# A conformer block with dilated attention on one Trainium2 core: hand order for the first norms, conv result split in pieces, early splits of the last projection

## The chip, the cores and the metric

The kernel runs on one core of one Trainium2 chip. A core has a matrix engine (TensorE, PE in the profile, with its weight loads as PEld), a vector engine (DVE), an activation engine (ACT), GpSimd (POOL) and SyncE (SP), whose queue issues nearly all transfers here. Each engine takes its instructions in order, and semaphores tie the engines together. The metric is the device time of one execution in microseconds (us), as the median of several runs. Lower is better.

## The reference

One layer of a block over 1024 tokens of width 1024, all in float32:

```
h = rms_norm(x, norm1_g);  z = h @ w_in            # glu 2048 | q 1024 | k 1024 | v 1024 | gates 2048
a = a_val * sigmoid(a_gate)                        # the two halves of glu
a = causal_depthwise_conv(a, conv_w, conv_b)       # width 31
y_a = silu(rms_norm(a, conv_norm_g)) @ w_conv_out
o = 16 heads of 64: softmax over windows (128,1), (512,4), (2048,16), merged by their sums
y_b = o @ w_attn_out
x = x + (g_a * y_a + g_b * y_b) @ w_out            # g_a, g_b: sigmoid of the gates
h = rms_norm(x, norm2_g);  u = causal conv of width 3 over h @ w_up   # 2 * 2816 channels
x = x + (silu(u_gate) * u_val) @ w_down
```

## The kernel before

**Splits.** TensorE gets each float32 operand as two parts in a faster format: a high part, which ACT copies (line 76), and a low part, source minus high part, which DVE subtracts (line 77). `split` (line 74) issues both. A product of two operands is three matmuls: high by high, high by low, low by high (lines 108 to 110, 125 to 127, 550 to 552, 703). `stage` (line 79) loads a weight piece of 128 x 1024 into one of four buffers (tag "raw"), `wsplit` (line 84) splits it into tags "whi" and "wlo" with four buffers each, and `wpiece` (line 90) does both.

**The order of the instructions.** The context is made with `schedule_with_timeline_sim=True` (line 855): while the kernel is built, instructions are put in order on each engine, and the order in which the program asks for them is only the priority. So an instruction asked for late may stand early in its engine's queue if its inputs and its buffer are free in the builder's model.

**First norms (lines 197 to 224).** The eight tiles of x (128 tokens x 1024) are loaded (line 204); two weight pieces are asked for after the fourth, g0 and v0 of the first channel tile (line 207), with their splits. The norm's weight g1 is loaded to all 128 partitions by one transfer on ACT's queue (line 200). For each tile: squares and their sum on ACT (line 221), `rstd_of` (line 98: one scalar step on DVE, line 100, and a power on POOL, line 101), scaling by the root and g1 on DVE (line 223), and `transpose_split` (line 183): two PSUM banks with four transposes each (line 190), each bank then split into hT. hT lies in four buffers of pool hb1: high and low part for each half of 512 tokens.

**Channel tiles (lines 227 to 238).** For each of eight tiles c: 48 matmuls of the gate columns (`glug`), a sigmoid, 48 of the value columns (`gluv`), and a product. All 48 of one go through both halves of the tokens. Then come q, k and v (lines 301 to 313), 24 columns of gates, the long convolution on DVE (line 253), its norm, and the store of the result to DRAM as `da` (line 340).

**Heads with side work (lines 345 to 470).** Sixteen heads, each in two halves. PE alternates between scores, transposes of the weights, and products with v; the weights' transposes are split by ACT and DVE as well (`flip`, line 396). `fill` (line 415) takes steps from a generator, `side_work` (line 346), and puts them between a head's instructions. One step is three matmuls of one k. The side work is the rest of the gate columns, the last four in two halves of 32 steps each, and then the projection of the conv result, w_co, eight columns by two halves. That projection reads aT, the split of `da`, and aT takes the buffers of hT half by half: the first half at the mark "half" of `gate_steps` (line 163), the second when all gates are done. Each `load_split` (line 165) loads and splits four pieces of 128 x 1024 at once (lines 350 and 352). The four weights of a group are asked for after them (line 354).

**Up projection and last projection.** The up projection runs over 22 tiles f (lines 655 to 659): `up_first` (line 557), `up_sums` (line 566), `up_rest` (line 623), which ends with a store to `dff` (line 653). The last projection (lines 664 to 804) reads it back in groups of two tiles (`gload`, line 673), loads w_down (`wload`, line 679), splits both (`gsplit`, line 686; `wsplit`) and multiplies (`mac`, line 696) in the seven products of a Strassen-like scheme. The operands of the first two groups go into two buffers named `early` (line 664) of pool hb2, under the tags that held the left operands of `up_first`.

Of the kernel before, what the change touches and what calls it, by code (L numbers as in the profile page):

```python
# [12 lines left out]
F32 = mybir.dt.float32  # L13
F32R = mybir.dt.float32r
# [6 lines left out]
P = 128  # L21
# [4 lines left out]
DH = 64  # L26
# [24 lines left out]
def block_kernel(ctx: ExitStack, tc: tile.TileContext, x, g1, g2, pack, mask,  # L51
# [13 lines left out]
    def bank_ps(name):  # L65
        return psB.tile([P, 512], F32, tag="B", name=name)
# [116 lines left out]
    def transpose_split(dst, src, tt):  # L183

        half, c0 = tt // 4, (tt % 4) * P
        for kk in range(2):
            ps = bank_ps(f"tp_{tt}_{kk}")
            for j in range(4):
                k = kk * 4 + j
                pe.transpose(ps[:, j * P : (j + 1) * P], src[:, k * P : (k + 1) * P], ident)  # L190
            psv = ps.rearrange("p (a b) -> p a b", a=4)
            hi = dst[0][half][:, kk * 4 : kk * 4 + 4, c0 : c0 + P]
            lo = dst[1][half][:, kk * 4 : kk * 4 + 4, c0 : c0 + P]
            split(hi, lo, psv)


    with tc.tile_pool(name="ph1", bufs=1) as p1:
        t4 = lambda name, dt=F32: p1.tile([P, 1024], dt, tag="t4", bufs=4, name=name)
        gb1 = p1.tile([P, D], F32, tag="csq", bufs=1, name="gb1")
        act.dma_start(gb1, bass.AP(tensor=g1.tensor, offset=g1.offset, ap=[[0, P], [1, D]]))  # L200
# [7 lines left out]
        sp.dma_start(pk, pack)  # L208
        make_identity(nc, ident)
        pool.memset(mhalf, -0.5)  # L210
        pool.memset(ones, 1.0)
        dve.tensor_tensor(out=qkg, in0=pk[:, C_QG : C_QG + 1], in1=pk[:, C_KG : C_KG + 1], op=ALU.mult)
        dve.tensor_scalar(qkg, qkg, DH ** -0.5, None, op0=ALU.mult)

        hT = hb_tiles(hb1, "hT")
        for tt in range(8):
            xx = xt[tt]
            xs = t4(f"xs_{tt}")
            ss = p1.tile([P, 1], F32, tag="ss", bufs=2, name=f"ss_{tt}")
            rs = p1.tile([P, 1], F32, tag="rs", bufs=2, name=f"rs_{tt}")  # L220
            act.activation(xs, xx, AF.Square, accum_out=ss)
            rstd_of(rs, ss, D, ss)
            dve.scalar_tensor_tensor(out=xs, in0=xx, scalar=rs, in1=gb1, op0=ALU.mult, op1=ALU.mult)
            transpose_split(hT, xs, tt)
# [3 lines left out]
        for c in range(8):  # L228
            a = p1.tile([P, CW - 1 + T], F32, tag="apad", bufs=10, name=f"apad_{c}")
            pool.memset(a[:, : CW - 1], 0.0)  # L230
            gp = big_ps(f"glug_{c}")
            gemm_ch(gp, wfirst[0] if c == 0 else wpiece(w_ch[8 + c], f"g{c}"), hT)
            sg = t4(f"sg_{c}")
            act.activation(sg, gp, AF.Sigmoid)
            vp = big_ps(f"gluv_{c}")
            gemm_ch(vp, wfirst[1] if c == 0 else wpiece(w_ch[c], f"v{c}"), hT)
            dve.tensor_tensor(out=a[:, CW - 1 :], in0=vp, in1=sg, op=ALU.mult)
            apad.append(a)

        sqacc = p1.tile([P, T], F32, name="sqacc")  # L240
# [104 lines left out]
    with tc.tile_pool(name="ph2", bufs=1) as p2:  # L345
        def side_work():
            for t in gates:
                if t == "half":
                    aT = hb_tiles(hb1, "aT")
                    load_split(aT, da, 0, "a")  # L350
                yield
            load_split(aT, da, 1, "a")
            for c0 in (0, 4):
                ws = [wpiece(w_co[c], f"co{c}") for c in range(c0, c0 + 4)]
                for half in range(2):
                    for c in range(c0, c0 + 4):
                        yp = bank_ps(f"ya_{c}_{half}")
                        yield from gemm_half(yp, ws[c - c0], aT, half)
                        ya = cst.tile([P, 512], F32, tag="f2", bufs=2, name=f"ya_{c}_{half}")
                        act.activation(ya, yp, AF.Copy)  # L360
                        sp.dma_start(dya[c][:, half * 512 : half * 512 + 512], ya)
# [249 lines left out]
    with tc.tile_pool(name="ph4", bufs=1) as p4:  # L611
# [52 lines left out]
    early = [hb2.tile([P, 3, 1024], F32R, tag=f"hb{a}1", name=f"early{a}") for a in range(2)]  # L664
    with tc.tile_pool(name="ph5", bufs=1) as p5_:
        HF, G = FT // 2, 2
        groups = [range(f, min(f + G, HF)) for f in range(0, HF, G)]
# [11 lines left out]
        def wload(k, j, fs, pl=p5_):  # L679
            raw = pl.tile([P, G * 512], F32, tag="wr" if pl is p5_ else "raw", bufs=4,  # L680
                          name=f"wr{k}{j}_{fs[0]}")[:, : len(fs) * 512]
            sp.dma_start(raw.rearrange("p (f d) -> p f d", d=512),
                         w_down[k * HF + fs[0] : k * HF + fs[-1] + 1, :, j * 512 : j * 512 + 512].rearrange("f p d -> p f d"))
            return raw

        def gsplit(src, name, dst=None):
            n = src.shape[1]
            if dst is not None:
                split(*dst, src)
                return dst  # L690
# [28 lines left out]
        for fs in groups:  # L719
            e = early.pop(0) if early else None  # L720
            g = gload(0, 0, fs, dst=None if e is None else e[:, 0].bitcast(F32))
# [21 lines left out]
        for fs in groups:  # L743
            s2, t2 = part("s2", fs), part("t2", fs)
            first, last = fs is groups[0], fs is groups[-1]
            a21, a22, a11 = wload(0, 1, fs), wload(1, 1, fs), wload(0, 0, fs, wp)
# [10 lines left out]
        for fs in groups:  # L757
            s2, t2 = part("s2", fs), part("t2", fs)
            first, last = fs is groups[0], fs is groups[-1]
            a12, a11, a21 = wload(1, 0, fs, wp), wload(0, 0, fs), wload(0, 1, fs)  # L760
# [16 lines left out]
        for fs in groups:  # L777
            s2, t2 = part("s2", fs), part("t2", fs)
            first, last = fs is groups[0], fs is groups[-1]
            a12, a22, b21 = wload(1, 0, fs, wp), wload(1, 1, fs), gload(1, 0, fs)  # L780
# [78 lines left out]
```

## Time and profile before

| what | value |
|---|---|
| median of 3 runs | 1812.32 us (1812.14 to 1815.67) |
| the profiled execution, its own time | 1811.43 us |
| its span, first to last instruction | 1809.6 us |
| mean granted TensorE clock | 0.991 |
| PE busy, 0 to 45 us | 31.64 us |
| PE busy, 90 to 600 us | 506.27 of 510 us |
| PE busy, 600 to 1140 us | 527.73 of 540 us |
| PE busy, 1140 to 1300 us | 150.66 of 160 us |
| PE busy, 1640 to 1809 us | 166.07 of 169 us |

How to read the profile: a row of a group names line, engine, operation, what it writes and reads, shapes and count, then busy us and the mean ns of one, then the idle time ahead of it and what ended it. A row of the order of time starts with the start in us and the duration; with a count behind x, the duration is that of the whole row. A row of a table of stretches gives the stretch, its length, then for PE, PEld, DVE, ACT and POOL the busy us and (x) the instructions begun, then the granted clock, the share of the transfer engines and GB/s. SPq and ACTq are the queues that issue transfers. Matmuls overlap, so a row's duration is longer than the distance between two.

### The profile page before, as it was taken

The numbers are of one execution on the slowest core, as the hardware profiler recorded it, in microseconds if no ns is written. First come the engines' busy times: TensorE is split into PE (matmuls) and PEld (weight loads), VectorE is DVE, ScalarE is ACT, GpSimd is POOL, SyncE is SP. The second block draws the span as 40 slices with busy tenths as digits, with TensorE's granted clock in tenths as the row PEclk, the third lists the DMA queues.
The fourth block names the chain that finished last, engine by engine and source line by source line (L and its number), as shares of the span: only waits on it lengthen the run. The fifth ranks groups of instructions, "written<-read, shape, count | busy, mean of one in ns | idle before, by whom it ended". The sixth has DMA issues, their size and how long they took to land.

```text
span 1809.6 us, 22474 instructions
## 1 busy us (share of the span) xinstructions
PE 1765.8 (98%) x8244; PEld 1461.9 (81%) x8244; DVE 1318.8 (73%) x1798; ACT 771.6 (43%) x1202; POOL 195.8 (11%) x197
## 2 busy tenths in 40 slices
PE   7999999999999999999999999989999999999999
PEld 5888888888887888887888878768888888878887
DVE  5999999999735655666654543787777777789863
ACT  4111132232245656666655332545444554543441
POOL 1000133133002122222210000210000000000000
PEclk9999999999999999999999999999999999999999
DMA  5111145345549456666527543313222222389851
GB/s 203 59 47 47 41 134 163 116 134 157 157 173 246 145 158 175 180 165 179 164 70 279 169 160 133 104 48 107 80 82 81 71 95 91 116 303 335 298 180 47
DMA packets 142063, 257.57 MB, mean 142 GB/s; under 512 B 11265, under 2 KB 60545, under 8 KB 141953
## 3 DMA queue, kind: packets, MB, share of 16 engines
q1 hardware_dynamic: 141808, 255.61, 43.8%
q8 instruction: 65, 1.06, 0.3%
q10 hardware_dynamic: 144, 0.52, 0.1%
q14 instruction: 46, 0.37, 0.1%
HBM read 190.03 MB, written 66.06 MB: 142 GB/s over the span
## 4 chain that ended last, share of the span: by engine, by line
PE 53%; DMA 4%; DVE 4%; issue 1%; ACT 1%; SPq 1%; POOLq 0%; POOL 0%; DVEq 0%; ACTq 0%
PE xz L550 5%; PE xz L551 5%; PE xz L552 5%; PE dx L703 5%; PE dy L703 5%; DMA gg<-dya 2%; PE pp L400 2%; PE y L550 2%; PE y L552 2%; PE y L551 2%; PE ya L108 2%; PE ya L109 2%; PE ya L110 2%; PE o L408 2%; PE wo L126 1%; PE wo L127 1%
## 5 line engine op out<-in xcount | busy, mean ns | idle before, releaser
L253 DVE SCALAR_TENSOR_TENSOR cacc<-apad,pk,cacc 128x1024 f32<-128x1024 f32 x240 | 297.7, 1274 | 0.7
L125 PE MATMUL qkv<-hi_qkv,hT 128*128 128x512 f32 x384 | 151.8, 396 | 0.0
L127 PE MATMUL qkv<-hi_qkv,hT 128*128 128x512 f32 x384 | 150.0, 391 | 0.0
L126 PE MATMUL qkv<-lo_qkv,hT 128*128 128x512 f32 x384 | 149.4, 390 | 0.0
L389 DVE CUSTOM_DVE_ANT_0 p<-s,m 128x128 f32<-128x128 f32 (+7 forms) x128 | 95.1, 750 | 62.7 <-PE pp L400 39.0
L77 DVE TENSOR_TENSOR pl<-pp,ph 128x512 fp32r<-128x512 f32 x192 | 103.1, 549 | 49.1 <-ACT ph L76 48.6
L393 POOL TENSOR_SCALAR p<-p,st 128x128 f32<-128x128 f32 (+7 forms) x128 | 94.9, 748 | 335.5 <-DVE st L392 211.9
L76 ACT ACTIVATE ph<-pp 128x512 fp32r<-128x512 f32 x192 | 91.3, 487 | 92.2 <-PE pp L400 89.3
L649 DVE SCALAR_TENSOR_TENSOR u<-u,pk 128x1023 f32<-128x1023 f32 (+1 forms) x88 | 112.3, 1279 | 18.9 <-ACT u L647 18.5
L101 POOL TENSOR_TENSOR rs<-ss,mhalf 128x8 f32<-128x8 f32 (+1 forms) x40 | 80.3, 2010 | 353.1 <-DVE ss L100 353.0
L391 ACT ACTIVATE p<-p,st 128x128 f32<-128x128 f32 (+7 forms) x128 | 99.0, 776 | 14.6 <-DVE st L389 12.9
L108 PE MATMUL gate<-hT,hi_gt 128*128 128x512 f32 x256 | 101.8, 398 | 0.0
L109 PE MATMUL gate<-hT,hi_gt 128*128 128x512 f32 x256 | 100.8, 394 | 0.0
L110 PE MATMUL gate<-hT,lo_gt 128*128 128x512 f32 x256 | 100.3, 393 | 0.0
L400 PE MATMUL pp<-ident,p 128*128 128x128 f32 x576 | 94.4, 277 | 0.0
L127 PEld LDWEIGHTS qkv<-hi_qkv,hT 128*128 128x128 f32 x384 | 72.0, 188 | 15.3
L126 PEld LDWEIGHTS qkv<-lo_qkv,hT 128*128 128x128 f32 x384 | 72.2, 188 | 14.5 <-DVE lo_qkv L77 0.3
L125 PEld LDWEIGHTS qkv<-hi_qkv,hT 128*128 128x128 f32 x384 | 72.2, 188 | 14.0
L400 PEld LDWEIGHTS pp<-ident,p 128*128 128x128 f32 x576 | 69.5, 142 | 10.0 <-issue 0.2
L384 PE MATMUL s<-kh,q 128*128 128x512 f32 (+1 forms) x192 | 69.7, 368 | 7.3 <-DVE st L389 4.8
L408 PE MATMUL o<-ph,v 128*128 128x512 f32 x192 | 73.1, 381 | 3.6 <-ACT ph L76 1.8
L409 PE MATMUL o<-pl,v 128*128 128x512 f32 x192 | 70.5, 369 | 1.6 <-DVE pl L77 1.5
(269 smaller groups left out, 4610.4 us busy)
## 6 DMA issues: line engine op xcount, KB each, us to landing
wr<-w_down SPq DMA_DIRECT2D x45, 512.0 KB, 5.7
gr<-dff SPq DMA_DIRECT2D x62, 256.0 KB, 5.2
raw_qkv<-w_qkv SPq DMA_DIRECT2D x24, 512.0 KB, 3.9
raw_uv<-w_up SPq DMA_DIRECT2D x22, 512.0 KB, 3.3
raw_ug<-w_up SPq DMA_DIRECT2D x22, 512.0 KB, 3.3
dff<-u SPq DMA_DIRECT2D x22, 512.0 KB, 2.6
dv<-v SPq DMA_DIRECT2D x16, 512.0 KB, 3.2
raw_gt<-w_ch SPq DMA_DIRECT2D x16, 512.0 KB, 4.8
```

The source lines that it names most:

```text
L108: pe.matmul(o, hi[:, k, :], ah[:, k, :], start=(k == 0), stop=False)
L109: pe.matmul(o, hi[:, k, :], al[:, k, :], start=False, stop=False)
L110: pe.matmul(o, lo[:, k, :], ah[:, k, :], start=False, stop=(k == KT - 1))
L125: pe.matmul(ps, ah, hi[:, k % 2, :], start=(k == 0), stop=False)
L126: pe.matmul(ps, ah, lo[:, k % 2, :], start=False, stop=False)
L127: pe.matmul(ps, al, hi[:, k % 2, :], start=False, stop=(k == KT - 1))
L253: dve.scalar_tensor_tensor(out=acc, in0=a[:, j : j + T], scalar=w(j), in1=acc, op0=ALU.mult, op1=ALU.add)
L400: pe.transpose(pp[:, qb * P : (qb + 1) * P], pts[qb][:, kt * P : (kt + 1) * P], ident)
L550: pe.matmul(o, wh[:, k, :], bh[:, k, :], start=(start and k == 0), stop=False, skip_group_check=not start)
L551: pe.matmul(o, wh[:, k, :], bl[:, k, :], start=False, stop=False, skip_group_check=not start)
L552: pe.matmul(o, wl[:, k, :], bh[:, k, :], start=False, stop=(k == 3), skip_group_check=not start)
L703: pe.matmul(banks[n], a[:, c], b[:, d], start=(start and i == 0 and m == 0), stop=(stop and i == nf - 1 and m == 2), skip_group_check=True)
```

## The change

It has three parts.

**First norms in a hand order.** The order of ACT, DVE and PE in this stretch is fixed by `tc.manual_schedule`. g1 is loaded as one row, multiplied by a row of ones on PE into two banks, and copied by DVE into gb1. All four squares of the first half come first; the scalar step of a tile stands after the scaling of the tile two before it, in the second half after the scaling of the tile one before. Transposes, high and low parts are issued bank by bank. The products of channel tile 0 are taken apart (`first_pair`): the first half of the tokens begins with k 0 to 3 as soon as the first banks of tiles 0 to 3 are split, and the transposes of tiles 4 to 7 stand between the products. Gate and value columns of one half share one two-bank PSUM tile. Sigmoid and product of tile 0 go by halves. The weights of channel tile 1 are asked for behind the last high and low part, and so are the two small instructions for qkg.

**Conv result in pieces.** A piece of the first half of aT is asked for at the mark and then every seventh step of side work; the pieces of the second half are asked for one ahead of each of the first four column products, behind the weights w_co.

**Early splits.** The loads and splits into `early` are asked for ahead of the last `up_rest`, no longer in the first pass of the last projection; `wload` and the groups move up with them.

The core of the diff:

```diff
-    def load_split(dst, src, half, name):
-        for k in range(0, KT, 2):
+    def load_split(dst, src, half, name, ks=range(0, KT, 2)):
+        for k in ks:
...
-        gb1 = p1.tile([P, D], F32, tag="csq", bufs=1, name="gb1")
-        act.dma_start(gb1, bass.AP(tensor=g1.tensor, offset=g1.offset, ap=[[0, P], [1, D]]))
+        g1r = p1.tile([1, D], F32, tag="csq", bufs=1, name="g1r")
+        act.dma_start(g1r, g1.unsqueeze(0))
...
-                wfirst = [wpiece(w_ch[8], "g0"), wpiece(w_ch[0], "v0")]
+                wfirst = [(c, n, stage(w_ch[c], n)) for c, n in ((8, "g0"), (0, "v0"))]
...
+        glu0 = [big_ps("glugv_0"), None]
+        third = big_ps("tp_2")
...
+        def both(tt, kk):
+            return high(tt, kk), low(tt, kk)
+        def first_pair(half, ks, passes, which):
+            o = glu0[half][:, which * 512 : which * 512 + 512]
+            for wa, ha in passes:
+                for k in ks:
+                    pe.matmul(o, wfirst[which][wa][:, k, :], hT[ha][half][:, k, :],
+                              start=(k == 0 and (wa, ha) == (0, 0)), stop=(k == 7 and (wa, ha) == (1, 0)))
...
+        HH, HL, LH = ((0, 0),), ((0, 1),), ((1, 0),)
+        with tc.manual_schedule(engines={ENG.Activation, ENG.DVE, ENG.PE}):
+            ps = [bank_ps(f"gb_{kk}") for kk in range(2)]
+            for kk in range(2):
+                pe.matmul(ps[kk], ones[0:1, :], g1r[:, kk * 512 : kk * 512 + 512], start=True, stop=True)
+            for tt in range(4):
+                squares(tt)
+            dve.tensor_copy(gb1[:, 0:512], ps[0])
+            spread1(0)
+            dve.tensor_copy(gb1[:, 512:1024], ps[1])
+            spread1(1)
+            for tt in range(4):
+                scaled(tt)
+                turned(tt)
+                if tt < 2:
+                    spread1(tt + 2)
+                if tt == 2:
+                    both(0, 0)
+            both(0, 1)
+            both(1, 0)
+            both(2, 0)
...
+            act.activation(hl[0][0], wraw[0], AF.Copy)
+            both(3, 0)
+            act.activation(hl[1][0], wraw[1], AF.Copy)
+            wlow(0)
+            wlow(1)
+            a, b = range(4), range(4, 8)
+            first_pair(0, a, HH, 0)
+            first_pair(0, a, HH, 1)
+            first_pair(0, a, HL + LH, 0)
+            first_pair(0, a, HL + LH, 1)
+            squares(4)
+            spread1(4)
+            both(1, 1)
+            both(2, 1)
+            both(3, 1)
+            squares(5)
+            scaled(4)
+            spread1(5)
+            first_pair(0, b, HH, 0)
+            turned(4)
+            first_pair(0, b, HH, 1)
+            squares(6)
+            scaled(5)
+            spread1(6)
+            turned(5)
+            first_pair(0, b, HL + LH, 0)
...
+            ends = both(7, 1)
+        for ks in (a, b):
+            for which in range(2):
+                first_pair(1, ks, HH + HL + LH, which)
...
+        with tc.issue_after(ends[0].ins), tc.issue_after(ends[1].ins):
+            wsecond = [wpiece(w_ch[9], "g1"), wpiece(w_ch[1], "v1")]
...
                 if t == "half":
                     aT = hb_tiles(hb1, "aT")
-                    load_split(aT, da, 0, "a")
+                    left = list(range(0, KT, 2))
+                    wait = 0
+                elif left:
+                    if wait == 0:
+                        load_split(aT, da, 0, "a", [left.pop(0)])
+                    wait = (wait + 1) % 7
                 yield
-            load_split(aT, da, 1, "a")
+            left = list(range(0, KT, 2))
             for c0 in (0, 4):
                 ws = [wpiece(w_co[c], f"co{c}") for c in range(c0, c0 + 4)]
                 for half in range(2):
                     for c in range(c0, c0 + 4):
+                        if left:
+                            load_split(aT, da, 1, "a", [left.pop(0)])
...
         for f in range(FT):
+            if f == FT - 1:
+                for a, fs in enumerate(groups[:2]):
+                    e = hb2.tile([P, 3, 1024], F32R, tag=f"hb{a}1", name=f"early{a}")
+                    for i, k in enumerate(fs):
+                        sp.dma_start(e[:, 0, i * 512 : i * 512 + 512].bitcast(F32), dff[k][:, 0:512])
+                    split(e[:, 1], e[:, 2], e[:, 0].bitcast(F32))
+                    early.append((e[:, 1], e[:, 2]))
             up_rest(f, *ready.pop(0))
...
-            mac(X, gsplit(g, f"b11_{fs[0]}", None if e is None else (e[:, 1], e[:, 2])), wsplit(w, f"a11_{fs[0]}"), len(fs), fs is groups[0], fs is groups[-1])
+            g = early.pop(0) if early else gsplit(gload(0, 0, fs), f"b11_{fs[0]}")
+            mac(X, g, wsplit(w, f"a11_{fs[0]}"), len(fs), fs is groups[0], fs is groups[-1])
```

The new helpers not shown are the old instructions under names: `squares` (line 221 of before), `spread1` (`rstd_of`), `scaled` (line 223), `turned` (two banks of transposes), `high` and `low` (the two halves of a split of one bank), `wlow` (the low part of a weight).

More of the change, by code (lines that the diff above doesn't have):

```diff
@@ L215, in block_kernel @@
         hT = hb_tiles(hb1, "hT")
[L216 to L224, printed above, removed]
+        glu0 = [big_ps("glugv_0"), None]
@@ new lines, in block_kernel, with squares, spread1 @@
+        third = big_ps("tp_2")
+        gb1 = p1.tile([P, D], F32, tag="sqacc", bufs=1, name="gb1")
+        xn = [t4(f"xs_{tt}") for tt in range(4)]
+        st1 = p1.tile([P, 2, 8], F32, name="st1")
+        tps = {}
+        def squares(tt):
+            if tt >= 4:
+                xn.append(t4(f"xs_{tt}"))
+            act.activation(xn[tt], xt[tt], AF.Square, accum_out=st1[:, 0, tt : tt + 1])
+        def spread1(tt):
+            rstd_of(st1[:, 1, tt : tt + 1], st1[:, 0, tt : tt + 1], D, st1[:, 0, tt : tt + 1])
@@ new lines, in scaled, with turned @@
+        def scaled(tt):
+            dve.scalar_tensor_tensor(out=xn[tt], in0=xt[tt], scalar=st1[:, 1, tt : tt + 1], in1=gb1,
+                                     op0=ALU.mult, op1=ALU.mult)
+        def turned(tt):
+            for kk in range(2):
+                ps = third[:, kk * 512 : kk * 512 + 512] if tt == 2 else bank_ps(f"tp_{tt}_{kk}")
+                for j in range(4):
+                    k = kk * 4 + j
+                    pe.transpose(ps[:, j * P : (j + 1) * P], xn[tt][:, k * P : (k + 1) * P], ident)
+                tps[tt, kk] = ps.rearrange("p (a b) -> p a b", a=4)
@@ new lines, in part, with high, low @@
+        def part(tt, kk, a):
+            half, c0 = tt // 4, (tt % 4) * P
+            return hT[a][half][:, kk * 4 : kk * 4 + 4, c0 : c0 + P]
+        def high(tt, kk):
+            return act.activation(part(tt, kk, 0), tps[tt, kk], AF.Copy)
+        def low(tt, kk):
+            return dve.tensor_tensor(out=part(tt, kk, 1), in0=tps[tt, kk], in1=part(tt, kk, 0).bitcast(F32),
+                                     op=ALU.subtract)
+        def both(tt, kk):
+            return high(tt, kk), low(tt, kk)
@@ L661, in block_kernel @@
     p4r_cm.__exit__(None, None, None)
-    early = [hb2.tile([P, 3, 1024], F32R, tag=f"hb{a}1", name=f"early{a}") for a in range(2)]
     with tc.tile_pool(name="ph5", bufs=1) as p5_:
-        HF, G = FT // 2, 2
-        groups = [range(f, min(f + G, HF)) for f in range(0, HF, G)]
         keep3 = {}
@@ L677, in gload, with gsplit @@
             return raw[:, : len(fs) * 512]
[L679 to L686, printed above, removed]
+        def gsplit(src, name):
             n = src.shape[1]
-            if dst is not None:
-                split(*dst, src)
-                return dst
             hi = p5_.tile([P, G * 512], F32R, tag="gh", bufs=4, name=f"gh_{name}")[:, :n]
```

82 lines of the change are left out of this document (56 added, 26 removed).

## The prediction

> **What bounds the kernel now.** I read the page first, then the waits of TensorE (PE), then a table of stretches, and last the order of time where PE stands still.
>
> ```profile
> span 1809.6 us, 22474 instructions
> ```
> and, from its first part,
>
> ```profile
> PE 1765.8 (98%) x8244; PEld 1461.9 (81%) x8244; DVE 1318.8 (73%) x1798; ACT 771.6 (43%) x1202; POOL 195.8 (11%) x197
> ```
> PE is busy for 1765.8 of 1809.6 us. An edit of order can win only in the 43.8 us of idle PE, and where PE is busy at a lower clock. The table says where these are (stretch, its length, busy us by engine, then PEclk):
>
> ```profile
> 0.00:45.00 45.00, 31.64 (x148) 25.62 (x149) 24.94 (x38) 22.08 (x38) 7.00 (x24) 0.92 0.53 204
> 90.00:600.00 510.00, 506.27 (x2342) 419.07 (x2342) 434.99 (x521) 149.49 (x223) 90.51 (x53) 0.99 0.42 129
> 1140.00:1300.00 160.00, 150.66 (x670) 122.31 (x669) 130.59 (x138) 84.50 (x107) 15.13 (x8) 0.98 0.24 83
> 1300.00:1600.00 300.00, 300.00 (x1325) 248.40 (x1324) 229.26 (x250) 147.67 (x175) 0.00 (x0) 1.00 0.27 92
> 1600.00:1640.00 40.00, 38.60 (x170) 31.29 (x169) 34.01 (x33) 16.41 (x17) 0.00 (x0) 1.00 1.05 403
> ```
> The first 45 us hold 13.36 us of idle PE. From 1140 to 1300 us lie 9.34 us, which the change does not touch. From 90 to 600 and from 1300 to 1600 us PE hardly waits, so time won ahead of them should travel through to the end.
>
> **The start (first norms).** In order of time, the idle time ahead in brackets:
>
> ```profile
> 5.99 1.06 ACT L221 ACTIVATE xs<-x 128x1024 f32<-128x1024 f32 x1 [3.55 <-DMA x<-x]
> 8.07 1.28 DVE L223 SCALAR_TENSOR_TENSOR xs<-x,rs,gb 128x1024 f32<-128x1024 f32 x1 [0.75 <-POOL rs L101]
> 9.41 4.03 PE L190 MATMUL tp<-ident,xs 128*128 128x128 f32 x16 [9.41 <-DVE ss L100]
> 10.57 0.60 ACT L76 ACTIVATE hT<-tp 128x512 fp32r<-128x512 f32 x1 [1.95 <-PE tp L190]
> 14.75 1.07 PE L190 MATMUL tp<-ident,xs 128*128 128x128 f32 x8 [1.30 <-DVE ss L100]
> 17.76 1.94 PE L190 MATMUL tp<-ident,xs 128*128 128x128 f32 x8 [1.94 <-DVE xs L223]
> 20.18 0.80 PE L108 MATMUL glug<-hT,hi_g 128*128 128x512 f32 x1 [0.48 <-ACT hT L76]
> 27.60 1.91 PE L190 MATMUL tp<-ident,xs 128*128 128x128 f32 x16
> 40.21 0.39 PE L109 MATMUL gluv<-hT,hi_v 128*128 128x512 f32 x1
> 42.02 0.39 PE L108 MATMUL gluv<-hT,hi_v 128*128 128x512 f32 x1
> 48.21 0.50 PE L108 MATMUL glug<-hT,hi_g 128*128 128x512 f32 x1
> ```
> PE waits for DVE between tiles, begins its products at 20.18 and reaches channel tile 1 at 48.21. From 40.21 to 42.02 lie eight steps: 0.227 us a matmul. The row at 27.60 is 16 transposes: (1.91 - 0.27) / 15, some 0.11 each. From 20.18 on, tile 0's 96 matmuls (21.8) and the last 32 transposes (3.5) make 25.3 us; they took 28.0. The rest is mostly half clock, which shows from 17 us on:
>
> ```profile
> 17.00:18.00 1.00, 0.24 (x2) 0.27 (x2) 1.00 (x2) 1.00 (x4) 0.12 (x1) 0.50 1.08 432
> ```
> What the new order costs comes from these groups and rows (in a group: busy us, mean ns of one; in the last row the us from issue to landing):
>
> ```profile
> L77 DVE TENSOR_TENSOR hT<-tp,hT 128x512 fp32r<-128x512 f32 x16 | 10.3, 682 | 3.7 <-ACT hT L76 3.7
> L101 POOL TENSOR_TENSOR rs<-ss,mhalf 128x1 f32<-128x1 f32 x8 | 5.3, 670 | 9.3 <-DVE ss L100 9.2
> L77 DVE TENSOR_TENSOR lo_g<-raw_g,hi_g 128x1024 fp32r<-128x1024 f32 x3 | 3.7, 1220 | 8.0 <-ACT hi_g L76 8.0
> L100 DVE TENSOR_SCALAR ss<-ss 128x1 f32<-128x1 f32 x8 | 1.1, 146 | 7.4 <-ACT xs L221 7.4
> L335 DVE COPY sqacc<-psr x2: 691/692/692, 507.9 to 518.6; 128x512 f32<-128x512 f32 x2
> 0.72 0.41 ACTq L200 DMA_DIRECT2D gb<-g  x1
> 506.43 0.61 PE L333 MATMUL psr<-dg,ones 128*128 128x128 f32 x4
> dff<-u SPq DMA_DIRECT2D x22, 512.0 KB, 2.6
> ```
> Removed: the transfer of gb1 to 128 partitions (512 KB) beside the x tiles; at the 432 GB/s of the row at 17 us it takes 1.2 us of all queues, so x tiles land up to 1.2 us sooner. Added: a 4 KB transfer, two matmuls that spread it over the partitions, two copies (2 x 0.69 on DVE). Those matmuls are not in the trace. By the row at 506.43 (two plain f32 matmuls of 128 columns are four records in 0.61, 0.11 each) 512 columns are two records of 0.43: between 1.7 us at full clock and 3.4 us at half clock for the pair. I take 3.4, as nothing ran before. Issued at 0.72 and landed by the quickest row of the page (2.6) the vector is there at 3.3; the matmuls end at 6.7, the second copy at 7.4, and after a scalar step the first scaling begins near 8.0, as before. A landing 2 us later would move the whole chain by 2: nothing covers it. PE has no other work until then; the squares run ahead on ACT meanwhile. On POOL the fill of the ones passes two small fills and the identity, which is not needed before 9 us: 0. SP's order of loads stays as it is.
>
> On DVE then come: four scalings (5.1), two scalar steps (0.3; their powers run on POOL under the next scaling) and one low part (0.7): the fourth scaling ends near 14.1. Its first four transposes and the reading cost 1.2 (9.41 to ACT's copy at 10.57 in the old order), its high part 0.6, so the first product starts near **16.3** instead of 20.18. The high part of the first weight lies on ACT ahead of that copy (the splits of whole weights take 1.06 there), under the fourth scaling; should the weight land after 14 us, the in-order ACT would hold back the copy, the first product and all of PE behind it. Six loads of 512 KB up to the second weight are 3.1 MB, some 7.3 us at 432 GB/s, so both land near 11 us and I cost this at nothing.
>
> From 16.3 PE owes the same 25.3 us. The order of DVE decides whether it gets them without gaps: from 14.1 to the end of the eighth scaling DVE owes 10 low parts (6.8), two weight low parts (2.4), four scalings (5.1), four scalar steps (0.6) and perhaps two bare waits for a power (0.8 each), 16.5, ending at 30.6. PE's work ahead of that tile's transposes (44 matmuls, 24 transposes) ends at 28.9. Behind a bare wait stand the low parts on DVE, and behind these PE's products. So PE waits 0 to 1.7; I take 1.0. Half clock costs 0 to 2.7 (what it costs now); I take 1.2. Tile 1 then starts at 43.8: **4.4 us gained**, between 2.2 (both at their worst) and 6.6 (neither). The splits for tile 1 now wait for the last low part (near 33); they need 2 x (1.06 + 1.22) = 4.6 us and PE has 48 matmuls (10.9) to cover them.
>
> The clock is the doubtful term. The transposes of 9.41 were followed by eight in 1.07 at 14.75 and, after pauses, eight in 1.94 at 17.76: transposes alone brought full clock, pauses took it back. [...]
>
> **The conv result in pieces.** The table and the order of time around both bursts:
>
> ```profile
> 760.00:780.00 20.00, 19.17 (x110) 16.18 (x109) 17.03 (x40) 16.07 (x33) 4.42 (x6) 1.00 0.70 225
> 780.00:800.00 20.00, 20.00 (x110) 17.07 (x109) 9.56 (x25) 9.97 (x24) 4.03 (x6) 1.00 0.48 135
> 810.00:820.00 10.00, 7.16 (x36) 6.08 (x35) 9.07 (x15) 9.14 (x15) 1.28 (x2) 0.79 0.99 317
> 820.00:830.00 10.00, 10.00 (x46) 8.18 (x45) 7.63 (x12) 6.06 (x11) 0.50 (x1) 0.87 0.66 223
> ```
> ```profile
> 760.03 3.91 ACT L76 ACTIVATE aT<-raw_a 128x1024 fp32r<-128x1024 f32 x4
> 810.35 3.89 ACT L76 ACTIVATE aT<-raw_a 128x1024 fp32r<-128x1024 f32 x4
> 811.43 4.63 DVE L77 TENSOR_TENSOR aT<-raw_a,aT 128x1024 fp32r<-128x1024 f32 x4
> 812.68 12.59 SPq L81 DMA_DIRECT2D raw_co<-w_co  x8
> 814.45 0.33 PE L408 MATMUL o<-ph,v 128*128 128x128 f32 x1 [1.30 <-ACT ph L76]
> 816.32 0.47 PE L409 MATMUL o<-pl,v 128*128 128x128 f32 x1 [1.54 <-DVE pl L77]
> ```
> Four splits back to back fill ACT for 3.9 and DVE for 4.6 us; the head's own splits queue behind them and PE waits 1.30 and 1.54. Then the clock drops: 36 and 46 matmuls start where 110 in 20 us is usual, 28 too few, at 0.18 us some 5 us. The first burst costs 0.83. At stake are 5.9 us. The four weights of the conv projection are even asked for after the second burst (812.68), since its pieces hold all four raw buffers; afterwards these weights come first. In pieces each split is 1.06 on ACT and 1.22 on DVE per seven or eight steps of side work; the gates' 32 steps took 50 us, so some 11 us lie between pieces. Ten steps follow the last first-half piece and eight the last second-half one, 12 us or more of cover. The loads go past the heads' fetches on SP; a blocked load would cost a head what waits on fetches cost at most. I take **4.5** (2 to 5.9), as eight lone splits may leave some tenths each.
>
> **The last projection.**
>
> ```profile
> L76 ACT ACTIVATE early<-early x2: 1060/1062/1063, 1573.8 to 1578.0; 128x1024 fp32r<-128x1024 f32 x2
> 1594.47 0.39 PE L703 MATMUL dx<-hi_a,early 128*128 128x512 f32 x1
> PE dx L703 <- ACT gh_t L76: 1.3, 1, 1.3
> ```
> Its first splits already run at 1573.8, 20 us ahead of use, and PE crosses into it without a pause. Asking earlier wins **0**. The 1.3 us wait lies in the second pass, behind transfers; another order of the queue may win or lose it: -1.4 to +1.4.
>
> **Sum.** 4.4 + 4.5 + 0 = 8.9 us. The profiled execution took 1811.43 (1.83 around its span), 0.9 below the median of 1812.32; from the median I forecast **1803.4**. By the bounds (2.2 + 2 - 1.4, and 6.6 + 5.9 + 1.4) this case reaches from 1798.4 to 1809.5.
>
> **Rivals.** All from 1812.3.
> - Half clock at the start: sixteen transposes and some fifteen first matmuls at double price cost all of the 2.7, all of the waits and 0.6 ahead of the first product: 1.6 gained there, 4.5 in the heads: 1806.2. For: the 0.50 rows after short pauses. Against: the row at 14.75.
> - The pieces only move the waits: 0 there, 4.4 at the start: 1807.9. Against: four splits at 760 cost only 0.83.
> - The start is given back further on, by DVE's long conv or a head's fetch: 1807.8. Against: 506.27 of 510 us PE-busy.
> - Neither works, since every wait returns in another place: 1812.3.
> - Slower: each lone piece stops its head, in-order ACT and DVE holding back the softmax for a full 1.06 + 1.22. Eight make 18.2, less 5.9 and 4.4: 1820.2. It decides from (5.9 + 4.4 + 3.6) / 8 = 1.7 us a piece. Against: the burst at 760 cost PE 0.2 a piece.
>
> **Chances.** Forecast 0.55; half clock 0.12; pieces move 0.10; given back 0.08; neither 0.08; slower 0.07. About 0.2% (3.6 us) is what a measurement tells from no change. Counting nearly all of the forecast and four fifths to two thirds of the next three as faster: 0.76 faster, 0.16 within, 0.08 slower. The range 1798.4 to 1810.5 leaves out the last two cases and little more.
>
> **What would show it.** First product by 17 us and tile 1 by 44.5 us; clock not at 0.50 between 18 and 23 us; between 755 and 850 us no PE wait over 1 us and no clock under 0.95; no change between 1560 and 1600 us. Wrong if DVE's wait for a power leaves PE idle past 2 us after 17 us, or if a lone split shows as a wait of PE above 1 us in the heads.

## The result, and the profile after

The changed kernel takes 1808.42 us (median of 15 runs, 1805.41 to 1813.15). The kernel before, run in turns with it, takes 1815.57 us (15 runs, 1812.14 to 1820.55; the 1812.32 of the prediction was a median of three). The ratio is 0.9966, with a 95% interval from 0.9955 to 0.9977: some 6 us faster (4.2 to 8.2); the two medians lie 7.15 apart. Two repeats gave 0.9970 (0.9959 to 0.9981) and 0.9971 (0.9960 to 0.9982). The forecast was 1803.4 us, 8.9 us below its median, with a range of 1798.4 to 1810.5. The time lies in the range; the gain of 8.9 lies above all three intervals, which end at 8.2, 7.4 and 7.3 us.

The profiled execution of after took 1811.24 us, 2.8 above its own median, so its span nearly equals the one before. Single executions lie up to 3 us below and 5 us above the median; what the change did has to be read stage by stage.

```profile
span 1809.5 us, 22485 instructions
```

**The start.** First the order of time of after's engines up to 45 us, in extracts (start, duration, what, and in brackets the idle time ahead with what ended it).

```profile
2.45 3.74 PE L255 MATMUL gb<-g1r,ones 1*128 1x512 f32 x4 [2.45 <-DMA g1r<-g]
4.07 1.06 ACT L212 ACTIVATE xs<-x 128x1024 f32<-128x1024 f32 x1 [1.52 <-DMA x<-x]
7.04 1.29 DVE L218 SCALAR_TENSOR_TENSOR xs<-x,st,gb 128x1024 f32<-128x1024 f32 x1
8.39 6.79 PE L226 MATMUL tp<-ident,xs 128*128 128x128 f32 x32 [2.19 <-DVE xs L218]
12.60 1.28 DVE L218 SCALAR_TENSOR_TENSOR xs<-x,st,gb 128x1024 f32<-128x1024 f32 x1
13.79 1.88 DVE L237 TENSOR_TENSOR hT<-tp,hT 128x512 fp32r<-128x512 f32 x3
14.49 1.05 ACT L280 ACTIVATE whi_g<-raw_g 128x1024 fp32r<-128x1024 f32 x1
15.43 0.59 ACT L234 ACTIVATE hT<-tp 128x512 fp32r<-128x512 f32 x1
16.08 1.21 PE L247 MATMUL glugv<-hT,whi_g 128*128 128x512 f32 x4 [0.89 <-ACT hT L234]
22.83 1.28 DVE L218 SCALAR_TENSOR_TENSOR xs<-x,st,gb 128x1024 f32<-128x1024 f32 x1 [0.71 <-POOL st L101]
27.35 1.27 DVE L218 SCALAR_TENSOR_TENSOR xs<-x,st,gb 128x1024 f32<-128x1024 f32 x1
41.58 0.39 PE L108 MATMUL glug<-hT,hi_g 128*128 128x512 f32 x1
```
The ones-matmuls took 3.74 us (3.4 was taken), but the short row landed at 2.45, so the first scaling stands at 7.04. The first product stands at 16.08, tile 1 begins at 41.58 in place of 48.21: 6.63 us won. Behind the fourth tile DVE has one bare wait for a power (0.71), and PE's rows show no wait behind it. Ahead of the first product, the copy of the first weight's high part (14.49) stands on ACT before the high part of the fourth tile (15.43), whose transposes had ended near 14.7. The table of stretches of after (length, busy us of PE, PEld, DVE, ACT, POOL with the instructions begun, granted clock, DMA share, GB/s):

```profile
0.00:45.00 45.00, 39.35 (x180) 30.88 (x181) 31.32 (x46) 26.76 (x42) 6.94 (x24) 1.00 0.57 209
16.00:45.00 29.00, 28.92 (x144) 24.18 (x145) 22.12 (x32) 17.30 (x28) 2.35 (x6) 1.00 0.40 137
750.00:850.00 100.00, 94.60 (x495) 78.57 (x495) 64.23 (x155) 63.45 (x134) 23.26 (x32) 0.97 0.66 192
810.00:820.00 10.00, 7.15 (x25) 5.65 (x25) 7.89 (x12) 6.59 (x13) 1.27 (x2) 0.66 0.89 290
1560.00:1600.00 40.00, 40.00 (x179) 33.11 (x178) 30.46 (x31) 22.60 (x26) 0.00 (x0) 1.00 0.50 161
```
From 16 us on PE is dense (28.92 of 29). Between 810 and 820 us nothing was won: 25 matmuls begin, where before had 36, and the clock stands at 0.66. The same work stands some 3 us earlier in after, so these two stretches do not hold quite the same; over the 100 us from 750 on it is 495 matmuls against 510 in before (row further down).

**The heads.** ACT's order of time in after, around both halves of the conv result, and under it PE's rows that follow:

```profile
755.57 3.91 ACT L76 ACTIVATE aT<-raw_a 128x1024 fp32r<-128x1024 f32 x4
...
806.84 1.06 ACT L76 ACTIVATE hi_co<-raw_co 128x1024 fp32r<-128x1024 f32 x1 [0.66 <-PE gate L109]
807.81 0.67 ACT L151 ACTIVATE gs<-gate,pk 128x512 f32<-128x512 f32 x1
808.38 2.94 ACT L76 ACTIVATE aT<-raw_a 128x1024 fp32r<-128x1024 f32 x3
...
814.57 1.06 ACT L76 ACTIVATE aT<-raw_a 128x1024 fp32r<-128x1024 f32 x1 [0.82 <-DMA raw_a<-da]
```
```profile
811.53 0.33 PE L531 MATMUL o<-ph,v 128*128 128x128 f32 x1 [1.09 <-ACT ph L76]
813.62 0.48 PE L532 MATMUL o<-pl,v 128*128 128x128 f32 x1 [1.76 <-DVE pl L77]
```
The pieces are asked for one by one, but on the chip they still run back to back: four in 3.91 us, then three in 2.94 and one more, whose load is late. PE waits behind them as before (1.09 and 1.76, where it was 1.30 and 1.54).

### The profile page after: what moved, and what is told of

Read it like the earlier page. It is cut to its first block, busy times and chain, and to the rows that moved or that the text cites. A ratio compares the mean times of both kernels' runs of the same rounds, so it can differ in the third digit from the quotient of the medians.

```text
span 1809.5 us, 22485 instructions
## 1 busy us (share of the span) xinstructions
PE 1771.3 (98%) x8248; PEld 1464.5 (81%) x8248; DVE 1320.5 (73%) x1801; ACT 771.8 (43%) x1203; POOL 194.5 (11%) x197
## 3 DMA queue, kind: packets, MB, share of 16 engines
q8 instruction: 65, 1.06, 0.2%
## 4 chain that ended last, share of the span: by engine, by line
PE 53%; DMA 4%; DVE 3%; issue 1%; ACT 1%; SPq 1%; POOLq 0%; POOL 0%; DVEq 0%; ACTq 0%
PE xz L673 5%; PE xz L674 5%; PE xz L675 5%; PE dx L832 5%; PE dy L832 5%; DMA gg<-dya 2%; PE pp L523 2%; PE y L673 2%; PE y L675 2%; PE y L674 2%; PE ya L108 2%; PE ya L109 2%; PE ya L110 2%; PE wo L126 2%; PE o L531 2%; PE wo L125 2%
## 5 line engine op out<-in xcount | busy, mean ns | idle before, releaser
L101 POOL TENSOR_TENSOR rs<-ss,mhalf 128x8 f32<-128x8 f32 x32 | 73.8, 2311 | 338.0 <-DVE ss L100 338.0
```

## The experiments

Each kernel ran in turns with the kernel before on the same chip, in three sets of runs. In these the kernel before had medians of 1812.08, 1811.93 and 1813.07 us (19, 28 and 23 runs).

**One part of the change at a time.** `start_only` is the kernel before with the first part of the diff, `pieces_only` with the second, `early_only` with the third.

> Only the first part: the first norms in hand order; conv result and early splits as before. Theory 1 (the start alone carries the gain): channel tile 1 starts near 41.6 us instead of 48.2, granted clock 1.00 from 16 to 32 us, and the median is 5 to 8 us below the kernel before. Theory 2 (the start's time is given back at the heads and the gain of the whole change comes from the pieces): tile 1 starts near 41.6 as well, but the median is within 2 us of before.

Measured: 1804.88 us, ratio 0.9961 (0.9948 to 0.9973), tile 1 at 41.84. In the third set the same kernel had 1806.60, ratio 0.9965 (0.9952 to 0.9977). The start alone brings all that the change brings, and probably more.

> Only the second part: the conv result asked for in pieces; start and early splits as before. Theory 1 (the request order is only a priority, the queues still hold the four splits of the first half back to back and three of the second): PE waits behind them for 2.5 to 3 us in all as before, and the median is within 2 us of before. Theory 2 (the prediction's term): no wait above 1 us between 755 and 850 us and a median 2 to 6 us below before.

Measured: 1815.50 us, ratio 1.0016 (1.0003 to 1.0028): slower by 0.5 to 5.1 us, which neither theory had forecast. The order of time of ACT and PE, and the stretch, show the way:

```profile
813.70 1.99 ACT L76 ACTIVATE aT<-raw_a 128x1024 fp32r<-128x1024 f32 x2
816.57 1.06 ACT L76 ACTIVATE aT<-raw_a 128x1024 fp32r<-128x1024 f32 x1 [0.88 <-DMA raw_a<-da]
817.53 0.26 ACT L76 ACTIVATE ph<-pp 128x128 fp32r<-128x128 f32 x1
...
817.85 0.33 PE L418 MATMUL o<-ph,v 128*128 128x128 f32 x1 [2.09 <-ACT ph L76]
```
```profile
750.00:850.00 100.00, 93.63 (x491) 77.07 (x489) 65.59 (x161) 64.67 (x136) 23.80 (x32) 0.97 0.67 195
```
ACT takes two splits, then stands 0.88 us before the third, whose load hasn't landed: the conv projection's weights are now asked for first and fill the four raw buffers. The head's own split (817.53) stands behind it, and PE waits 2.09. In these 100 us 491 matmuls begin, 19 fewer than in before (the row is quoted further down): by estimate some 3.6 us, at the 0.19 each of that row (96.19 us by 510).

> Only the third part: the first splits of the last projection asked for ahead of the last up tile. Theory 1 (these splits already stood early in the queues, the order of every engine comes out as before): 0, so this run also shows how far two equal programs lie apart, some 0.1 to 0.2 per cent. Theory 2 (the splits move and the last projection's first waits go): 1 to 1.5 us below before.

Measured: 1812.37 us, ratio 1.0004 (0.9995 to 1.0012). The third part does nothing: on every engine the instructions stand in the same order as before.

**Truly spread.** If the burst is what costs, pieces that stand apart in the queues must win. `spread` is the changed kernel in which each piece is also held behind the latest split of a head, on ACT and on DVE (`split` now returns its two instructions, and `issue_after` makes what follows depend on them):

```diff
+        latest = []
+        def behind(make):
+            with tc.issue_after(latest[0].ins), tc.issue_after(latest[1].ins):
+                return make()
...
-                        load_split(aT, da, 0, "a", [left.pop(0)])
+                        behind(lambda: load_split(aT, da, 0, "a", [left.pop(0)]))
...
-                            load_split(aT, da, 1, "a", [left.pop(0)])
+                            behind(lambda: load_split(aT, da, 1, "a", [left.pop(0)]))
...
-            split(ph[:, c], pl[:, c], pp[:, c])
+            latest[:] = split(ph[:, c], pl[:, c], pp[:, c])
```

> The changed kernel, with each piece of the conv result held behind the split of the head's latest flip on ACT and DVE, so that the eight pieces really stand apart in the queues (7 to 16 instructions between them on ACT). Theory 1 (the four splits back to back make PE wait and lose its clock): the waits of 1.1 and 1.8 us near 810 go, no clock below 0.95 between 755 and 830 us, and the median is 2 to 5 us below the changed kernel's (9 to 12 below before). Theory 2 (a lone split holds its head up as well, the waits only move): waits of a few tenths at each of eight places with the same sum of 3 us, and the median is within 1.5 us of the changed kernel's.

Measured: 1800.40 us, ratio 0.9942 (0.9929 to 0.9954): faster than both kernels, 11.7 us below the kernel before and 4.5 below the start alone of the same set. The group of the pieces in after, then in spread (count, shortest, median and longest in ns, first and last start), and below it the stretch of spread:

```profile
L76 ACT ACTIVATE aT<-raw_a x8: 1042/1062/1070, 755.6 to 814.6; 128x1024 fp32r<-128x1024 f32 x8
```
```profile
L76 ACT ACTIVATE aT<-raw_a x8: 1046/1052/1063, 755.4 to 849.1; 128x1024 fp32r<-128x1024 f32 x8
...
750.00:850.00 100.00, 97.53 (x531) 81.30 (x531) 70.78 (x169) 68.13 (x141) 22.63 (x31) 1.00 0.63 190
```
The eight splits now reach over 94 us, no clock falls, and 531 matmuls begin where after had 495. PE's longest wait in spread for a split of ACT or DVE between 745 and 850 us is 0.5 (total, times, longest):

```profile
PE gate L108 <- DVE pl L77: 0.5, 1, 0.5
```

The spread pieces could owe this to the earlier start beside them. So `spread_only` is the kernel before with the pieces held in the same way, and its old start:

> The kernel before with one edit: the eight pieces of aT are asked for one by one and each is held on ACT and DVE behind the latest split of the flip, so that they stand apart in the queues; the start and the last projection stay as they were. Burst theory (what stands back to back costs PE its turns and its clock): between 755 and 850 us no granted clock under 0.95, the longest PE wait there under 1 us each, and 3 to 5 us below the kernel before. Rival, that the gain of the spread pieces over the run with the new start alone came from the earlier start beside it, or that the waits only move to another place: within 1.5 us of the kernel before.

Measured: 1808.20 us, ratio 0.9976 (0.9967 to 0.9984), 3.7 us faster. The stretch in before, then in spread_only:

```profile
750.00:850.00 100.00, 96.19 (x510) 80.53 (x509) 68.97 (x168) 67.68 (x141) 24.40 (x33) 0.97 0.69 198
```
```profile
750.00:850.00 100.00, 97.69 (x530) 81.68 (x529) 70.45 (x170) 67.49 (x143) 25.42 (x34) 1.00 0.64 190
```
Twenty more matmuls at the 0.19 us of before's row (96.19 by 510) make an estimate of 3.8 us, about the whole gain; by the start of the projection w_out (table below) it is 2.9 in these two profiles. The rival, that waits only move or that the gain came from the earlier start, fell.

**What is left of ACT's waits.** The conv weights now go ahead of the second half's pieces, and in after ACT's split of them waits for PE's gate columns. The waits of the stretch from 745 to 850 us (total, times, longest), in after and in spread:

```profile
ACT hi_co L76 <- PE gate L109: 2.9, 2, 2.2
```
```profile
ACT hi_co L76 <- PE gate L109: 1.7, 1, 1.7
```
`spread_co` holds the four weights back too:

```diff
+                    if wait in (11, 18, 25):
+                        ws0.append(behind(lambda: wpiece(w_co[len(ws0)], f"co{len(ws0)}")))
...
+                    ws = ws0 + [behind(lambda: wpiece(w_co[3], "co3"))]
```

> The changed kernel with the pieces spread, and the four first weights of w_co held behind the flip's splits as well, three of them asked for among the gates' last steps. Theory that ACT's waits at these weights for PE's gate (2.2 us in all in the changed kernel) still hold up PE: 0.5 to 1.5 us below the run with the pieces spread, 10 to 13 us below the kernel before, and no such wait of ACT left. Rival, that these waits are beside the path once the pieces stand apart: within 0.7 us of the run with the pieces spread, so 9 to 11 us below the kernel before.

Measured: 1802.36 us, ratio 0.9948 (0.9936 to 0.9960), and no wait of `hi_co` for a gate is left in its list (one of 1.9 us stands at ACT's next work on the gates, `gs`, instead). The theory, that the wait still holds up PE, fell: nothing was won. Of the rival's two figures one came true, 9.6 us below the kernel before. The other, within 0.7 us of spread, did not: by their own kernels before, spread_co lies 2.1 us behind. The two ran in different sets and their intervals overlap, so whether holding the weights costs something stays open.

**What of the start carries the gain.** `old_g1` keeps the hand order but fetches g1 to 128 partitions in one 512 KB load again:

```diff
-        g1r = p1.tile([1, D], F32, tag="csq", bufs=1, name="g1r")
-        act.dma_start(g1r, g1.unsqueeze(0))
+        gb1 = p1.tile([P, D], F32, tag="sqacc", bufs=1, name="gb1")
+        act.dma_start(gb1, bass.AP(tensor=g1.tensor, offset=g1.offset, ap=[[0, P], [1, D]]))
...
-                pe.matmul(ps[kk], ones[0:1, :], g1r[:, kk * 512 : kk * 512 + 512], start=True, stop=True)
```

> The new start alone, but with g1 fetched again as one broadcast load of 128 rows in place of the 4 KB row, the two ones-matmuls and their two copies: what is left is the order written out by hand and the later first weights. Theory that the order carries the gain: x lands about 1.2 us later, the first product of the two matrices stands at 17 to 18 us in place of 16.1, tile 1 begins at 42.5 to 44 us (41.8 with the row), and the time is 4 to 6.5 us below the kernel before. Rival, that the short load and the matmuls carry it: tile 1 at 45 us or later and 0 to 3 us below the kernel before.

Measured: 1808.20 us, ratio 0.9977 (0.9968 to 0.9987). Its order of time at the start:

```profile
5.93 1.06 ACT L211 ACTIVATE xs<-x 128x1024 f32<-128x1024 f32 x1 [3.48 <-DMA x<-x]
...
10.07 4.66 PE L225 MATMUL tp<-ident,xs 128*128 128x128 f32 x24 [10.07 <-DVE xs L217]
14.95 1.17 PE L225 MATMUL tp<-ident,xs 128*128 128x128 f32 x8 [0.21 <-DVE xs L217]
16.85 1.20 PE L246 MATMUL glugv<-hT,whi_g 128*128 128x512 f32 x4 [0.74 <-ACT hT L233]
...
42.38 0.39 PE L108 MATMUL glug<-hT,hi_g 128*128 128x512 f32 x1
```
x lands 1.86 us later than in after, yet tile 1 begins only 0.80 later: the marks speak for the order, which keeps 5.8 of the 6.6 us. The time, 3.7 us below before, lies between the two theories. So it was run again beside the start alone, together with the changed kernel, which had also been repeated once:

> The changed kernel once more, on the chip and beside the runs of the other kernels of this call. Theory that the pieces as they are cost a little on top of the new start's gain: 4.5 to 6.5 us below the kernel before, where the new start alone was 7.1 below. Rival, that the pieces cost nothing beside the new start: 7 to 8 us below.

Measured: 1805.53 us, ratio 0.9970 (0.9959 to 0.9981): 6.4 below before, at the upper end of what the first theory said.

> The new start alone once more, beside the two kernels that it is to be compared with. Theory: tile 1 at 41.6 to 42 us and 6 to 8 us below the kernel before.

> The new start with g1's broadcast load once more. Theory that the short load is worth what it moves the mark of tile 1, some 0.5 us: within 1.5 us of the new start alone of this call, so 5 to 7.5 us below the kernel before. Rival, that its 3.5 us of the two earlier calls are real: 2 to 4.5 us below the kernel before.

> The changed kernel once more, beside the new start alone. Theory that the pieces as they stand in the queues cost something on top of the new start: 1 to 3 us above the new start alone of this call. Rival, that beside the new start they cost nothing: within 1 us of it.

Measured side by side: `start_2` 1806.60, 6.5 below before, with tile 1 at 41.33, a little ahead of what was expected; `old_g1_2` 1809.22, ratio 0.9978 (0.9970 to 0.9987), 3.9 below; `after_3` 1808.44, ratio 0.9971 (0.9960 to 0.9982), 4.6 below and 1.8 above start_2, as its first theory had it, but with overlapping intervals. For old_g1_2 the numbers are the rival's, and my "worth what it moves the mark" fell. Where the time goes shows in the marks. The table gives where groups begin in each profile, in us, and the median against that of before in the same set:

| kernel | q, k, v | first aT split | conv projection | w_out | median against before |
|---|---|---|---|---|---|
| before | 200.7 | 760.0 | 820.0 | 1064.0 | |
| early_only | 201.0 | 760.7 | 820.7 | 1064.8 | +0.3 |
| pieces_only | 201.4 | 760.9 | 823.8 | 1068.6 | +3.4 |
| spread_only | 201.2 | 763.6 | 817.9 | 1061.1 | -3.7 |
| start_only, start_2 | 194.2, 193.6 | 755.9, 754.6 | 815.6, 814.6 | 1059.0, 1057.6 | -7.2, -6.5 |
| old_g1, old_g1_2 | 194.7, 195.1 | 756.2, 756.7 | 817.3, 818.9 | 1059.7, 1063.2 | -3.7, -3.9 |
| after, after_again, after_3 | 193.9, 194.1, 193.8 | 755.6, 754.5, 754.3 | 817.8, 815.8, 815.9 | 1061.6, 1059.2, 1059.3 | -7.2, -6.4, -4.6 |
| spread | 193.6 | 755.4 | 809.7 | 1052.9 | -11.7 |
| spread_co | 193.8 | 757.1 | 811.2 | 1054.6 | -9.6 |

old_g1 begins q, k and v 1.0 us behind the start alone (194.9 against 193.9, means of two), and loses another 2.0 between there and the conv projection (818.1 against 815.1). In the heads the two kernels' queues differ: about 30 lines in a comparison of ACT's 1052 copies, table loads and transfers, two of them g1's load, the rest in the heads from 662 us on, though the program asks for the heads in the same way. So this run is no clean trial of the load. About 1 us of it lies at the start; whether the 2 us in the heads come from that other order was not tried and stays open (in old_g1_2 alone PE also waits 1.66 us for a split of ACT at 818.33).

The same table gives the pieces' price in the changed kernel. From the first aT split to the conv projection it takes 61.7 us in after (mean of three profiles), 59.8 in the start alone (two): 1.9 us lost, and 1.8 by the start of w_out. The medians alone do not show it: after_3 and start_2 lie 1.8 apart with overlapping intervals, and after and start_only lie equally far below the kernel before.

## Why the prediction was right, and where only by luck

The direction and the range held; the gain came out a fifth to two fifths smaller than forecast. Two terms were off, in opposite directions: 4.4 + 4.5 + 0 was forecast; the runs show 6.5 to 7.2 for the start, then some 1.9 lost, then 0. That the sum came near is luck.

**The start: mechanism right, size too small.** First product at 16.3 forecast, 16.08 measured; PE's 25.3 us of work took 25.5 (16.08 to 41.58). The allowances on top, 1.0 for DVE's waits and 1.2 for half clock, did not occur: 43.8 less 2.2 is 41.6, where tile 1 stands. It is the bound of 6.6, "neither". DVE came through since it stood ahead of what was worked out: the eighth scaling ended near 28.6 in place of 30.6, with one bare wait, and low parts in a row take 1.88 for three, not three times 0.68.

That the first product came so near to its forecast is in part luck. Its terms (14.1 + 1.2 + 0.6) make 15.9, not 16.3. The first scaling stood at 7.04, not 8.0. And the high part of the first weight, put at nothing, did not run under the fourth scaling, which ended at 13.88, but from 14.49 on, and the fourth tile's copy waited behind it for some 0.7 us.

**The clock: right answer from an accidental row.** The matmul row of after runs over all 32 transposes (6.79 us from 8.39); the rows of their weight loads stand apart by tile. In before, eight loads in 0.86 go with the eight transposes in 1.07 at 14.75, and eight in 1.57 with those in 1.94 at 17.76, where the clock reads 0.50 (17 to 18 us). In after, the four tiles of the first half:

```profile
8.38 1.57 PEld L226 LDWEIGHTS tp<-ident,xs 128*128 128x128 f32 x8 [3.76 <-DVE xs L218]
10.40 1.57 PEld L226 LDWEIGHTS tp<-ident,xs 128*128 128x128 f32 x8 [0.45 <-DVE xs L218]
12.13 1.57 PEld L226 LDWEIGHTS tp<-ident,xs 128*128 128x128 f32 x8 [0.16 <-DVE xs L218]
13.99 0.96 PEld L226 LDWEIGHTS tp<-ident,xs 128*128 128x128 f32 x8 [0.29 <-PE tp L226]
```
Eight loads take 1.57 in the first three groups and 0.96 in the fourth, so the faster rate was there before the first product: in after within 5.6 us of the first group, in start_2 by the third group, 3.9 us after its first (1.57 at 8.45, 0.86 at 12.32). In old_g1, which has no ones-matmuls ahead, the fourth group takes 0.96 too. But the row argued from (1.07 at 14.75) was one execution's. In early_only, whose instructions stand in the order of before, that group took 1.94, its loads 1.57:

```profile
14.69 1.94 PE L190 MATMUL tp<-ident,xs 128*128 128x128 f32 x8 [1.30 <-DVE ss L100]
22.28 0.63 PE L108 MATMUL glug<-hT,hi_g 128*128 128x512 f32 x1
...
18.00:23.00 5.00, 4.52 (x14) 3.19 (x13) 5.00 (x11) 4.88 (x11) 1.10 (x2) 1.00 0.90 353
```
A product of 512 columns takes 0.63 there, not 0.39. In before, early_only and pieces_only, with the old order, PE pauses for 1.30 us ahead of the third group and for 1.06 to 1.94 ahead of the fourth; the fourth took 1.94 in all three, the third 1.07, 1.94 and 1.94. In all nine profiles of the new start the fourth group's eight loads took 0.95 or 0.96; the weight loads stood idle for at most 1.00 us ahead of each group but the first there, against 1.44 to 2.15 ahead of the third and the fourth in before and early_only. The products from 16.08 on take 1.21 for the first four and 1.07 to 1.09 for the next fours in after, where before and early_only have 0.63 to 0.80 for each of their first. The half-clock rival fell.

**The pieces: the step that failed** is "some 11 us lie between pieces". It read the order in which the program asks as the order on the queue, although that order is only a priority here. The burst was rightly priced at 4.5: spread_only won 3.7 and spread, over the start alone, 4.5 (1804.88 to 1800.40). But the edit didn't take the burst away: four of the eight pieces still ran in 3.91 us and three in 2.94, PE waited 1.09 and 1.76 where the prediction's own sign was no wait over 1 us, and the term of 4.5 became a loss of some 1.9. The nearest rival, that the pieces only move the waits, had a chance of 0.10 and a gain of 0 in the heads; that the pieces would not part at all was not among the rivals. The hope set on the weights going first also failed: they took the raw buffers, and the second half's loads came late (0.88 in pieces_only, 0.82 in after). The slower rival, a lone piece stopping its head, fell: in spread each piece is alone, and PE's longest wait there for a split of ACT or DVE is the 0.5 shown above. Its other half, ACT held back in order, did occur, but by a load that was late.

**The early splits: right.** PE is busy for 40.00 of 40 us from 1560 on, before and after, and the wait of 1.3 us in the second pass is still 1.3 in early_only. The row of before, beside that of after further up:

```profile
1560.00:1600.00 40.00, 40.00 (x178) 33.12 (x177) 30.36 (x31) 22.78 (x26) 0.00 (x0) 1.00 0.49 159
```

**Given back later?** Not for good. The 6.6 us at tile 1 are 6.8 at q, k and v (200.7 to 193.9). With the start alone, against before and early_only, whose order is the same (means of two each), 5.1 us are left at the first aT split and 6.1 at w_out, and its medians end 7.2 and 6.5 below. In the changed kernel the pieces take their part on top, as told.

## What to carry to other kernels

When a builder orders the queues, an edit of what is asked for when is only a wish: look up in the new queue where the instruction stands, and hold it there by a dependence if the gap is what matters. Here four splits in a row on ACT and DVE made the head behind them wait, and PE with it, at a price of some 4 us (3.7 in spread_only against before, 4.5 in spread against the start alone); with the same splits apart from each other, PE's longest wait for a split between 745 and 850 us was 0.5 us (spread). And a forecast of two terms is tested by running each alone: the sum here was near since one error covered the other.

## What the runs showed of the hardware

- **The clock fell after two short pauses in one execution, and not in another.** In after two pauses, 1.09 and 1.76 us with one matmul of 0.33 between, were followed by the first of these stretches of 5 us. In after_again the same two pauses came (1.1 and 1.7), and the second row shows the same stretch:

```profile
815.00:820.00 5.00, 5.00 (x16) 3.89 (x16) 3.02 (x4) 2.41 (x4) 0.15 (x1) 0.58 0.80 297
```
```profile
815.00:820.00 5.00, 4.64 (x19) 3.59 (x20) 1.97 (x4) 0.41 (x1) 0.00 (x0) 1.00 0.57 205
```
  The durations agree with the clock: products of 512 columns take 0.63 to 0.78 behind the pauses in after; in after_again those of the conv projection, from 815.8 us on, take 0.39 to 0.50. The lowest stretch of 5 us between 810 and 825 us reads 0.57 in before, 0.64 in early_only, 0.52 in pieces_only, 0.80 and 0.66 in start_only and start_2, 0.75 and 0.66 in old_g1 and old_g1_2; after_again and after_3 read 1.00 over the 100 us from 750 on, and the longest product of the projection is 0.50 in both. What decides is not shown. The longest pause ahead of the fall was 1.76 us in after, 1.54 in before and 2.09 in pieces_only. So the clock alone is not the price of the pieces: the two profiles without the fall also take 61.3 and 61.7 us from the first aT split to the conv projection, where the start alone takes 59.8.
- **From 18 to 23 us the granted clock disagreed with the durations.** It reads 1.00 for early_only between 18 and 23 us (row above) and 0.50 for before in the same stretch, with the same number of matmuls begun (14); the first products take 0.79 or 0.80 and 0.63 in both, so here the durations are the safer reading.

```profile
18.00:23.00 5.00, 4.52 (x14) 3.19 (x14) 5.00 (x10) 4.88 (x12) 1.10 (x2) 0.50 0.89 356
```
- **One program scatters.** From the start of w_out to the last projection the three profiles of the changed kernel took 532.7, 530.7 and 533.8 us, with only the early splits of the change in between, which early_only shows to be nothing. A single execution can't show a gain of 3 us at its end; a mark early in it can (tile 1 begins within 0.3 us in the three).
